# Differences of halves moved between the phases of a Strassen-like second MLP product, a residual update shared out over three doubled phases, and two loads of the first product moved by two steps

## The chip, the cores and the metric

One core of a Trainium2 chip runs the whole program. The metric is the device time of one execution in microseconds. Before the change it is 2566.15 us, the median of three runs (2564.7 to 2566.99). This kernel's runs differ by about 0.1% from each other.

## The reference, cut to what matters

The reference is one layer of an encoder over 2048 tokens of width 1024, in float32: a mixer of two attention kinds, then an MLP with a squared ReLU. The change lies in the MLP alone.

```python
h = rmsnorm(x, g_norm2[l]) * (1.0 + sc2) + sh2
x = x + gt2 * (jnp.square(jax.nn.relu(h @ w1[l])) @ w2[l])
```

`w1` is 1024 by 4096 and `w2` 4096 by 1024. Call `h @ w1` the first product, its squared ReLU the hidden layer, and the product with `w2` the second product.

## The kernel before, in words

**Numbers and tiles.** TensorE multiplies in pairs of float32r parts: each operand is split into a high and a low part (a cast on ScalarE, then a subtraction on VectorE), and each product is three matmuls (`mm3`). Both MLP products use a fast block scheme with seven block products in place of eight, numbered 1, 5, 6, 3, 7, 2, 4 in the order in which they run. The price is sums and differences of blocks, which run on VectorE. Tokens come in two halves (`mb` 1, then 0), each with two groups of 512 (`odd` 1 and 0).

**Steps.** The MLP is one list `steps`. A step is twelve matmuls in the first product (`First`) and in a plain phase (`Second`), six in a doubled phase (`Outer`). Everything that TensorE doesn't do is put into `jobs` by `at(n, job)`: job `n` is written out just ahead of step `n`. Before each step the loop (line 1978) also splits operands for later steps, as long as the eight tiles of `opp` suffice. Each engine then works its own instructions off in that order; the DMA queue of SyncE does so too, so that a DMA that waits holds up all that are written behind it. A table of step numbers, written by hand, thus sets the order on VectorE and in the DMA queue.

**The first product, `mb` 0.** For each of 16 column pairs `j` there are seven steps (a period). VectorE splits the next operands (`opw`), forms three sums of weight blocks for the next pair in temporary tiles (`ts`), combines four finished blocks (`cp`, `ca`, `cb`, `ce`), and prepares sums of `w2` for later phases (`wt`). For `j` below 8 it also makes four differences between the two token halves, for the block products 3, 7, 2 and 4. `other(i)` (line 1560) loads the other half's block from `scr_hid` into a temporary tile `to`; `keep` (line 1551) subtracts in place and stores the tile to `scr_hid` two steps later. Temporary tiles (`temp`) come from a pool of seven; a `ts` of the next period takes the memory of a `to` of the last one, and so waits until that `to` has been stored. Up to the eighth period an update of the residual also runs for the other half (`xu`: load a row of `scr_x`, add, store), in the two tiles of `rp`.

**The second product, `mb` 0.** It runs as: a plain phase for block product 1 (16 steps), doubled phase 7, a plain phase for 6 (16 steps), and doubled phases 5, 2, 3 and 4. A doubled phase takes one of the seven block products and applies the scheme a second time inside it: seven parts of eight steps, in the order 1, 5, 6, 3, 7, 2, 4. For each step VectorE subtracts the low part of one operand `opr`, and in every second step one `ol`. Its right operands `r` (four tiles for each part, `half` and `half_sum`, lines 1790 and 1796) are loaded for parts 1, 5, 3 and 2, and computed as differences for parts 6, 7 and 4: `6 = 3 - 5`, `7 = 6 - 1`, `4 = 2 - 6`. For doubled phase 5 part 5 is a difference as well (`5 - 1`). At the end of a part VectorE adds the finished sums from PSUM into rows of the residual (`txo`, `cxo`): four such additions where the phase serves two outputs (7 and 5), two elsewhere. `update` (line 1641) adds the sums of the plain phases to rows that no doubled phase finishes (`txu`): load, add six steps later, store three steps later.

**The numbers in the plan.** `plan["load"]` and `plan["sum"]` (lines 1916 to 1932) give for each part the step of the first of its four tiles and the gap between them. They are made for the phase that comes next: `f` is the first step of the phase just laid out, `e` the step behind its last one. In the first plan `f` is the plain phase for 1, so `f + 16` is the first step of doubled phase 7. In the plan that doubled phase 7 makes for doubled phase 5, `e` is the first step of the plain phase for 6 and `e + 16` that of doubled phase 5.

Of the kernel before, what the change touches and what calls it, by code (L numbers as in the profile page):

```python
# [79 lines left out]
def encoder_kernel(ctx, tc, xT, c, g1, g2, w_in, w_rest, gqk, bias, w_o, w1, w2, w_ada, b_ada, out):  # L80
# [1215 lines left out]
    if True:  # L1296
# [37 lines left out]
        def at(n, job):  # L1334
            jobs.setdefault(n, []).append(job)
# [228 lines left out]
        def second_sums(j, step):  # L1564

            t = []

            def load():
                t.append(raw_pair([P, 2, 2, TB], F32, f"w2s_{j}"))
                for s in range(2):  # L1570
                    sp.dma_start(t[0][:, s].rearrange("p r n -> p (r n)"), w2[2 * j + s])

            def out(i, dst, a, b, op):
                tile = {nm: t[0][:, s, r, :] for nm, s, r in (("11", 0, 0), ("21", 0, 1), ("12", 1, 0), ("22", 1, 1))}
                column_sum(dve, tile[dst], tile[a], tile[b], op)
                later.add(2, lambda: sp.dma_start(scr_s[i - 1 if i < 7 else 0, j // 2][:, j % 2, :], tile[dst]))

            at(step - (6 if j else 0), load)
            sums = ((5, "22", "21", "22", ALU.add), (7, "21", "11", "21", ALU.subtract))
            sums += ((6, "11", "22", "11", ALU.subtract), (3, "12", "12", "11", ALU.subtract))  # L1580
            for n, x in enumerate(sums):
                at(step + n + (0 if j else 3), lambda x=x: out(*x))
# [51 lines left out]
        def weigh(x, a, n):  # L1634
            dve.scalar_tensor_tensor(x, a, mod[:, 5 * KT + n : 5 * KT + n + 1], x, op0=ALU.mult, op1=ALU.add)

        def rows_of(t, mb, n, odd):
            tb = 2 * mb + odd
            return t[n * P : (n + 1) * P, tb * TB : (tb + 1) * TB]

        def update(mb, r, odd, loads, adds, home=None, last=False):

            xs = {}

            def fetch(n):
                xs[n] = x = (home or temp)(f"xu{mb}_{r}{odd}_{n}")
                sp.dma_start(x, scr_x[2 * mb + odd, HK * r + n])

            def add(n):
                x, row = xs[n], HK * r + n  # L1650
                weigh(x, Second.whole["s", n], row)
                dst = rows_of(out, mb, row, odd) if last else scr_x[2 * mb + odd, row]
                later.add(3, lambda: sp.dma_start(dst, x))

            for n in range(HK):
                at(loads[n], lambda n=n: fetch(n))
                at(adds[n], lambda n=n: add(n))

        def plain(mb, i):

            f = len(steps)
            steps.extend(Second(mb, i, j) for j in range(NP))
            if i == 6:
                spread = lambda *ns: [f + n for n in ns]
                update(mb, 0, 1, spread(0, 1, 2, 8), spread(4, 5, 6, 12))
            return f
# [27 lines left out]
        def narrow_sums(i, k, step):  # L1694

            t = []
            r, s = {2: (0, 1), 4: (1, 1)}[i]

            def load():
                for a in range(2):  # L1700
                    t.append(temp(f"wn{i}_{k}_{a}"))
                    sp.dma_start(t[a], w2[2 * (HP * a + k) + s][:, r * TB : (r + 1) * TB])

            def sums(pr, dst, a, b, op):
                v = {nm: t[h][:, c * CN : (c + 1) * CN] for nm, h, c in (("11", 0, 0), ("12", 1, 0), ("21", 0, 1), ("22", 1, 1))}
                column_sum(dve, v[dst], v[a], v[b], op)
                later.add(2, lambda: sp.dma_start(scr_t[i, pr][:, k, :], v[dst]))

            at(step - 4, load)
            todo = ((5, "22", "21", "22", ALU.add), (7, "21", "11", "21", ALU.subtract))  # L1710
            todo += ((6, "11", "22", "11", ALU.subtract), (3, "12", "12", "11", ALU.subtract))
            for n, x in enumerate(todo):
                at(step + n, lambda x=x: sums(*x))
# [154 lines left out]
        for mb in (1, 0):  # L1868
            begin = len(steps)
            steps += [First(mb, j, i) for j in range(NP) for i in OUTER]  # L1870
            end = len(steps)
            for j in range(NP):
                f = steps[begin + 7 * j]
                if mb:
                    second_sums(j, begin + 7 * j + 2)
                    if j >= HP:
                        narrow_sums(2, j - HP, begin + 71 + 5 * (j - HP))
                else:
                    outer_sums((7, 5, 3, 4)[j // 4], j % 4, begin + 7 * j - 2)
                    if j < HP:  # L1880
                        for i, n in ((3, 2), (2, 5), (7, 2), (4, 5)):
                            at(begin + 7 * j + n, lambda i=i, f=f: f.other(i))
                if j > mb:
                    at(begin + max(7 * j - 13, 2 if mb else -6), f.load)
                if j > mb or mb and j:
                    for m in range(4):
                        at(begin + (m + 1 if mb and j == 1 else 7 * j - 9 + (m if j > 1 else 0)), lambda f=f, m=m: f.fetch(m))
            if mb:
                norm2(1, begin + 18)
                norm2(0, begin + 48)  # L1890
                for k in range(HK):
                    begins = end + 6 * k
                    pieces = right_blocks(0, k, kept if k % 2 else temp)
                    for n, m in ((0, 0), (4, 4), (5, 5), (6, 6), (7, 7), (8, 7), (9, 7), (10, 7), (11, 7), (12, 7)):
                        at(begins + n, pieces[m])
                for i in PLAIN:
                    plain(1, i)
                for n in range(end, len(steps), 2):
                    at(n - 7 - max(0, end + 4 - n) // 2, steps[n].load)
                rest = len(steps)  # L1900
                lent = lambda nm: rp.tile([P, TB], F32, tag="r", name=nm)
                for n, (r, odd) in enumerate(((0, 0), (1, 1), (1, 0))):
                    at_row = rest + 3 + 16 * n
                    update(1, r, odd, range(at_row, at_row + 16, 4), range(at_row + 4, at_row + 20, 4), lent)
            else:
                at(begin - 8, steps[begin].load)
                at(begin - 6, steps[begin].fetch)

        def plain_loads(f, leads):
            for m in range(0, NP, 2):  # L1910
                at(f + m - (leads.pop(0) if leads else 7), steps[f + m].load)

        f = plain(0, 1)
        plain_loads(f, [9, 9, 9, 8, 8, 8])
        e = len(steps)
        plan = {"load": {1: (f - 3, 1), 5: (f + 2, 2), 3: (f + 10, 2), 2: (f + 18, 2)}}
        plan["sum"] = {6: (f + 16, 2), 7: (f + 21, 2), 4: (f + 44, 2)}
        for i in DOUBLE:
            f = outer(i, plan)
            e = len(steps)  # L1920
            if i == 7:
                plain_loads(plain(0, 6), [12, 11, 11, 11, 9, 8])
            spread = lambda *ns: [f + n for n in ns]
            if i == 2:
                update(0, 0, 0, spread(18, 22, 26, 30), spread(24, 28, 32, 36))
                update(0, 1, 1, spread(36, 40, 44, 48), spread(42, 46, 50, 54))
            if i == 3:
                update(0, 1, 0, spread(12, 16, 20, 24), spread(17, 21, 25, 29), None, True)
            plan = {"load": {1: (f + 22, 2), 5: (f + 17, 2), 3: (f + 30, 2), 2: (f + 46, 2)}}
            plan["sum"] = {6: ({7: e + 1, 5: e - 4}.get(i, f + 38), 2), 7: (e + (8 if i == 7 else 16), 2), 4: (e + (16 if i == 7 else 26), 2)}  # L1930
            if i == 7:
                plan["sum"][5] = (f + 31, 2)

        blocks = [right_blocks(1, k, kept if k else temp) for k in range(HK)]

# [104 lines left out]
```

## Time and profile before

| what | number |
|---|---|
| median of three runs | 2566.15 us |
| the profiled execution, its own time | 2567.03 us |
| its span, first to last instruction | 2565.3 us |
| TensorE busy (matmuls) | 2523.2 us, 98% |
| TensorE weight loads busy | 2094.1 us, 82% |
| VectorE busy | 2054.8 us, 80% |
| ScalarE busy | 1509.6 us, 59% |
| GpSimd busy | 747.5 us, 29% |
| DMA of SyncE, share of 16 engines | 80.4% |
| granted TensorE clock, mean | 0.999 |

All recorded operations have line L42, that of the helper which keeps them in program order, so the profile is read by tile names, not by lines. Times are given from the start of the span. A busy share tells what an engine did on average; how much a stage loses is read from the stage itself, by the time that it takes against the time of its matmuls when nothing holds them up. The MLP's first product for `mb` 0 begins at 1757 us, its second product at 2075 us, and the last matmul ends at 2561 us.

### The profile page before, as it was taken

To read this page: it belongs to the slowest core of one execution; us is meant where nothing else is said; L and a number is where in the kernel's file an instruction comes from. 1 tells how busy PE (TensorE), PEld (TensorE's weight loads), DVE (VectorE), ACT (ScalarE), POOL (GpSimd) and SP (SyncE) were. 2 spreads that over 40 slices of the span, in tenths; PEclk is the share of its full clock that TensorE was granted. 3 is DMA by queue.
4 is the path that set the end of the run, shared out by engine and by line. 5 is a ranking of instruction groups with operands and counts; after the bars stand their busy time and mean duration, and the time that the engine had idled before them with its cause. 6 is when DMAs were issued, how large, how long until landed. Compare 5 with 4: busy or idle time off the path is not lost.

```text
span 2565.3 us, 39482 instructions
## 1 busy us (share of the span) xinstructions
PE 2523.2 (98%) x12388; PEld 2094.1 (82%) x12388; DVE 2054.8 (80%) x3593; ACT 1509.6 (59%) x2893; POOL 747.5 (29%) x1128
## 2 busy tenths in 40 slices
PE   9999999999999999999999999999999999999999
PEld 7888888888888888887988888888778887787777
DVE  7656767887789879998768777789777659899998
ACT  6333435668866686666745555575445546466665
POOL 4330144776776667776710000000000000000000
PEclk9999999999999999999999999999999999999999
DMA  9879979789977788866787879987998886868892
GB/s 364 325 296 361 341 280 296 212 236 289 278 250 234 226 262 271 258 208 198 227 332 246 309 268 316 347 320 244 324 325 289 270 338 263 321 254 291 282 314 81
DMA packets 305105, 714.66 MB, mean 279 GB/s; under 512 B 32512, under 2 KB 91904, under 8 KB 293248
## 3 DMA queue, kind: packets, MB, share of 16 engines
q1 hardware_dynamic: 303600, 707.43, 80.4%
q10 hardware_dynamic: 1296, 4.72, 0.5%
q8 instruction: 98, 1.61, 0.3%
q14 instruction: 111, 0.91, 0.1%
HBM read 485.00 MB, written 227.02 MB: 278 GB/s over the span
## 4 chain that ended last, share of the span: by engine, by line
PE 71%; DVE 14%; DMA 7%; ACT 3%; issue 3%; POOL 1%; SPq 0%; DVEq 0%; ACTq 0%; POOLq 0%
PE ps L42 19%; PE pt L42 11%; PE ps_s L42 10%; PE acc L42 6%; PE wt L42 6%; PE pf L42 4%; PE z L42 4%; PE po L42 4%; DVE opr L42 3%; PE pq L42 3%; DVE r L42 2%; DVE p L42 2%; DMA scr_t<-wt 1%; PE cz L42 1%; DMA scr_hid<-to 1%
## 5 line engine op out<-in xcount | busy, mean ns | idle before, releaser
L42 PE MATMUL ps<-h,opw 128*128 128x512 f32 x1512 | 358.6, 389 | 0.0
L42 ACT CAST wth<-wt 128x512 fp32r<-128x512 f32 (+3 forms) x544 | 257.1, 483 | 167.7 <-PE wt L42 158.4
L42 POOL TENSOR_TENSOR b<-p 128x512 f32<-128x512 f32 (+1 forms) x320 | 292.5, 914 | 167.8 <-DVE p L42 93.0
L42 DVE TENSOR_TENSOR wtl<-wt,wth 128x512 fp32r<-128x512 f32 (+3 forms) x544 | 291.0, 547 | 58.1 <-ACT wth L42 56.3
L42 PEld LDWEIGHTS ps<-h,opw 128*128 128x128 f32 x1512 | 283.7, 188 | 58.8
L42 PE MATMUL ps_s<-h,opw 128*128 128x512 f32 x1152 | 278.5, 391 | 11.0 <-DVE cp L42 8.1
L42 PE MATMUL pt<-w,ht 128*128 128x512 f32 x1248 | 288.2, 391 | 0.0
L42 PEld LDWEIGHTS pt<-w,ht 128*128 128x128 f32 x1248 | 233.0, 188 | 47.7
L42 DVE TENSOR_TENSOR_SCAN p<-z,p,zero 128x512 f32<-128x512 f32 x192 | 245.7, 1281 | 25.6 <-ACT z L42 18.5
L42 PEld LDWEIGHTS ps_s<-h,opw 128*128 128x128 f32 x1152 | 215.2, 188 | 59.8 <-DVE cp L42 11.0
L42 ACT CAST opr<-r 128x512 fp32r<-128x512 f32 x280 | 174.2, 623 | 146.0 <-PE ps L42 69.7
L42 PE MATMUL ps<-opr,ol 128*128 128x512 f32 x960 | 223.6, 391 | 2.3 <-DVE opr L42 1.9
L42 PE MATMUL acc<-wth,v 128*128 128x512 f32 (+3 forms) x544 | 220.9, 410 | 0.0
L42 PEld LDWEIGHTS ps<-opr,ol 128*128 128x128 f32 x960 | 179.2, 188 | 44.2 <-DVE opr L42 5.3
L42 DVE TENSOR_TENSOR opr<-r,opr 128x512 fp32r<-128x512 f32 x280 | 185.8, 686 | 18.3 <-ACT opr L42 17.0
L42 ACT ACTIVATE z<-z 128x512 f32<-128x512 f32 (+1 forms) x320 | 166.5, 521 | 55.4 <-PE z L42 49.0
L42 PE MATMUL z<-k,q 128*128 128x512 f32 (+3 forms) x640 | 185.6, 372 | 7.7 <-DVE p L42 7.0
L42 PE MATMUL acc<-wtl,v 128*128 128x512 f32 (+3 forms) x544 | 185.7, 348 | 0.0
L42 PE MATMUL ps_s<-opr,ol 128*128 128x512 f32 x720 | 172.9, 394 | 4.7 <-DVE opr L42 3.9
L42 PE MATMUL ps<-oph,opv 128*128 128x512 f32 x768 | 176.0, 390 | 0.6 <-DVE oph L42 0.2
L42 PE MATMUL wt<-ident,b 128*128 128x128 f32 x1088 | 171.4, 273 | 0.9 <-DVE p L42 0.6
L42 PEld LDWEIGHTS ps<-oph,opv 128*128 128x128 f32 x768 | 143.9, 188 | 32.2 <-DVE oph L42 1.2
(215 smaller groups left out, 4875.1 us busy)
## 6 DMA issues: line engine op xcount, KB each, us to landing
r<-scr_hid SPq DMA_DIRECT2D x80, 512.0 KB, 7.3
q<-scr_q SPq DMA_DIRECT2D x128, 256.0 KB, 5.2
w<-in_w_dram SPq DMA_DIRECT2D x64, 512.0 KB, 5.8
k<-scr_k SPq DMA_DIRECT2D x240, 128.0 KB, 4.4
v<-scr_v SPq DMA_DIRECT2D x120, 256.0 KB, 4.1
wa<-in_w_ada_dram SPq DMA_DIRECT2D x48, 512.0 KB, 6.2
ow<-scr_wo SPq DMA_DIRECT2D x24, 1024.0 KB, 6.0
l<-scr_t SPq DMA_DIRECT2D x20, 1024.0 KB, 7.9
```

The source lines that it names most:

```text
L42: return lambda *x, **y: self.tc.keep_in_program_order(f(*x, **y))
```

## The change

It alters numbers in the table and moves two calls.

- First product: the loads for differences 3 and 7 are put two steps later (step 4 of the period in place of step 2).
- First plan: the loads for parts 5 and 3 and the differences for parts 6 and 7 of doubled phase 7 are put earlier.
- Plan for doubled phase 5: its own part-5 differences move from step 31 of doubled phase 7 to the first steps of the plain phase for 6; parts 6, 7 and 4 follow later.
- Updates: one row group (`odd` 1) moves from doubled phase 2 to doubled phase 3, another (`odd` 0) from 3 to 4.

```diff
-                        for i, n in ((3, 2), (2, 5), (7, 2), (4, 5)):
+                        for i, n in ((3, 4), (2, 5), (7, 4), (4, 5)):
                             at(begin + 7 * j + n, lambda i=i, f=f: f.other(i))
...
-        plan = {"load": {1: (f - 3, 1), 5: (f + 2, 2), 3: (f + 10, 2), 2: (f + 18, 2)}}
-        plan["sum"] = {6: (f + 16, 2), 7: (f + 21, 2), 4: (f + 44, 2)}
+        plan = {"load": {1: (f - 3, 1), 5: (f + 1, 2), 3: (f + 6, 2), 2: (f + 18, 2)}}
+        plan["sum"] = {6: (f + 12, 2), 7: (f + 15, 2), 4: (f + 44, 2)}
...
             if i == 2:
                 update(0, 0, 0, spread(18, 22, 26, 30), spread(24, 28, 32, 36))
-                update(0, 1, 1, spread(36, 40, 44, 48), spread(42, 46, 50, 54))
+                pass
             if i == 3:
-                update(0, 1, 0, spread(12, 16, 20, 24), spread(17, 21, 25, 29), None, True)
+                update(0, 1, 1, spread(18, 22, 26, 30), spread(24, 28, 32, 36))
+            if i == 4:
+                update(0, 1, 0, spread(2, 6, 10, 14), spread(8, 12, 16, 20), None, True)
...
-            plan["sum"] = {6: ({7: e + 1, 5: e - 4}.get(i, f + 38), 2), 7: (e + (8 if i == 7 else 16), 2), 4: (e + (16 if i == 7 else 26), 2)}
+            plan["sum"] = {6: ({7: e + 8, 5: e - 4}.get(i, f + 38), 2), 7: (e + (20 if i == 7 else 16), 2), 4: (e + (30 if i == 7 else 26), 2)}
             if i == 7:
-                plan["sum"][5] = (f + 31, 2)
+                plan["sum"][5] = (e + 1, 2)
```

TensorE's and ScalarE's instructions keep their order. Three places show what moves.

The DMA queue of SyncE in the fourth period (`j` = 3) of the first product, as one piece of the difference. `to0_3_1_3` is the tile of period 3 for difference 3; a row that begins with `scr_hid0` is the store of a finished difference, here of period 2.

```order
 L42 DMA xu1_11_1_21769<-scr_x3_5_217 128x512
-L42 DMA to0_3_1_3_21771<-scr_hid1_3_1_16881 128x512
-L42 DMA to0_3_1_7_21773<-scr_hid1_7_1_16913 128x512
-L42 DMA scr_hid0_7_1_16849<-to0_2_1_7_21593 128x512
-L42 DMA scr_hid0_3_1_16817<-to0_2_1_3_21591 128x512
+L42 DMA scr_hid0_7_1_16849<-to0_2_1_7_21632 128x512
+L42 DMA scr_hid0_3_1_16817<-to0_2_1_3_21630 128x512
 L42 DMA scr_t7_3_16772<-wt7_3_21503 128x2x256
 L42 DMA scr_hid0_4_1_16825<-to0_2_1_4_21658 128x512
+L42 DMA to0_3_1_3_21809<-scr_hid1_3_1_16881 128x512
+L42 DMA to0_3_1_7_21811<-scr_hid1_7_1_16913 128x512
 L42 DMA scr_x3_4_216<-xu1_11_0_21654 128x512
```

The two loads go behind the stores of differences 7, 3 and 4; what follows keeps its place.

VectorE in doubled phase 7, part 7, before the change, and then with it. `r5_5_1` is a part-5 difference for doubled phase 5, `r7_4_2` a part-4 difference for phase 7 itself.

```order
L42 TENSOR_TENSOR opr7_7_4_24666<-r7_7_2_24365,opr7_7_4_24666 128x512
L42 TENSOR_TENSOR ol7_7_4_24669<-l7_7_0_24512,ol7_7_4_24669 128x512
L42 TENSOR_TENSOR r7_4_2_24672<-r7_2_2_24321,r7_6_2_24294 128x1024
L42 TENSOR_TENSOR opr7_7_5_24686<-r7_7_2_24365,opr7_7_5_24686 128x512
L42 TENSOR_TENSOR r5_5_1_24498<-r5_5_1_24498,r5_1_1_24566 128x1024
L42 TENSOR_TENSOR opr7_7_6_24696<-r7_7_3_24396,opr7_7_6_24696 128x512
L42 TENSOR_TENSOR ol7_7_6_24699<-l7_7_0_24512,ol7_7_6_24699 128x512
L42 TENSOR_TENSOR r7_4_3_24702<-r7_2_3_24352,r7_6_3_24323 128x1024
L42 TENSOR_TENSOR opr7_7_7_24712<-r7_7_3_24396,opr7_7_7_24712 128x512
L42 TENSOR_TENSOR r5_5_2_24523<-r5_5_2_24523,r5_1_2_24589 128x1024
```

```order
L42 TENSOR_TENSOR opr7_7_4_24665<-r7_7_2_24288,opr7_7_4_24665 128x512
L42 TENSOR_TENSOR ol7_7_4_24668<-l7_7_0_24512,ol7_7_4_24668 128x512
L42 TENSOR_TENSOR r7_4_2_24671<-r7_2_2_24329,r7_6_2_24248 128x1024
L42 TENSOR_TENSOR opr7_7_5_24685<-r7_7_2_24288,opr7_7_5_24685 128x512
L42 TENSOR_TENSOR opr7_7_6_24694<-r7_7_3_24315,opr7_7_6_24694 128x512
L42 TENSOR_TENSOR ol7_7_6_24697<-l7_7_0_24512,ol7_7_6_24697 128x512
L42 TENSOR_TENSOR r7_4_3_24700<-r7_2_3_24356,r7_6_3_24277 128x1024
L42 TENSOR_TENSOR opr7_7_7_24710<-r7_7_3_24315,opr7_7_7_24710 128x512
```

Two of the four part-5 differences for phase 5 stood in these rows, the others just ahead of and behind them; all four now stand in the plain phase for 6.

VectorE in doubled phase 5, at the change from part 5 to part 6, before the change and then with it. `cxo` adds finished sums from PSUM.

```order
L42 TENSOR_TENSOR opr5_5_7_25490<-r5_5_3_24548,opr5_5_7_25490 128x512
L42 TENSOR_TENSOR opr5_6_0_25507<-r5_6_0_25035,opr5_6_0_25507 128x512
L42 TENSOR_TENSOR ol5_6_0_25510<-l5_6_0_25403,ol5_6_0_25510 128x512
L42 TENSOR_TENSOR opr5_6_1_25521<-r5_6_0_25035,opr5_6_1_25521 128x512
L42 TENSOR_TENSOR opr5_6_2_25530<-r5_6_1_25078,opr5_6_2_25530 128x512
L42 TENSOR_TENSOR ol5_6_2_25533<-l5_6_0_25403,ol5_6_2_25533 128x512
```

```order
L42 TENSOR_TENSOR r5_7_3_25474<-r5_6_3_25299,r5_1_3_24619 128x1024
L42 TENSOR_TENSOR opr5_5_7_25482<-r5_5_3_24548,opr5_5_7_25482 128x512
L42 TENSOR_TENSOR opr5_6_0_25499<-r5_6_0_25184,opr5_6_0_25499 128x512
L42 TENSOR_TENSOR ol5_6_0_25502<-l5_6_0_25391,ol5_6_0_25502 128x512
L42 TENSOR_TENSOR opr5_6_1_25513<-r5_6_0_25184,opr5_6_1_25513 128x512
L42 TENSOR_TENSOR opr5_6_2_25522<-r5_6_1_25223,opr5_6_2_25522 128x512
L42 TENSOR_TENSOR ol5_6_2_25525<-l5_6_0_25391,ol5_6_2_25525 128x512
L42 TENSOR_TENSOR r5_4_0_25528<-r5_2_0_24864,r5_6_0_25184 128x1024
```

Doubled phase 5 now holds its four part-7 differences, which stood in the plain phase for 6, and its part-4 differences stand some steps later than before.

## The prediction

> **What bounds the kernel now.** I read the page first: TensorE is busy for 98% of the span at full clock, so what can be won is the little that it idles. Then I cut the MLP's last part into stretches and asked for each one's length. In the rows below stand the stretch, its length, the busy time of TensorE, its weight loads, VectorE, ScalarE and GpSimd, the clock, the DMA share and GB/s. After the page's row, the first seven are periods of the first product (`j` = 3 to 9), then come the plain phase for 1, doubled phase 7, the plain phase for 6, and doubled phases 5, 2, 3 and 4.
>
> ```profile
> PE 2523.2 (98%) x12388; PEld 2094.1 (82%) x12388; DVE 2054.8 (80%) x3593; ACT 1509.6 (59%) x2893; POOL 747.5 (29%) x1128
> ...
> 1814.49:1836.40 21.91, 19.67 (x86) 15.61 (x84) 16.25 (x26) 10.23 (x18) 0.00 (x0) 1.00 0.91 315
> 1836.40:1859.24 22.84, 19.69 (x86) 15.61 (x84) 16.82 (x27) 10.22 (x18) 0.00 (x0) 1.00 0.99 347
> 1859.24:1879.97 20.73, 19.35 (x85) 15.69 (x84) 16.91 (x27) 10.01 (x18) 0.00 (x0) 1.00 0.99 340
> 1879.97:1900.35 20.38, 19.35 (x86) 15.69 (x85) 16.82 (x27) 10.01 (x18) 0.00 (x0) 1.00 0.91 294
> 1900.35:1921.36 21.01, 19.33 (x86) 15.69 (x84) 16.25 (x26) 10.02 (x18) 0.00 (x0) 1.00 0.99 335
> 1921.36:1941.55 20.19, 19.33 (x85) 15.69 (x84) 16.14 (x27) 10.01 (x18) 0.00 (x0) 1.00 0.98 338
> 1941.55:1960.59 19.04, 19.04 (x85) 15.77 (x84) 13.45 (x22) 10.23 (x18) 0.00 (x0) 1.00 0.81 276
> 2075.00:2118.52 43.52, 43.52 (x193) 36.05 (x193) 23.04 (x36) 21.29 (x38) 0.00 (x0) 1.00 0.88 346
> 2118.52:2202.04 83.52, 80.37 (x337) 62.22 (x337) 82.17 (x121) 50.76 (x87) 0.00 (x0) 1.00 0.75 283
> 2202.04:2245.90 43.86, 43.82 (x193) 35.96 (x193) 35.48 (x51) 18.27 (x32) 0.00 (x0) 1.00 0.83 325
> 2245.90:2322.06 76.16, 76.16 (x337) 63.06 (x337) 72.37 (x112) 50.46 (x86) 0.00 (x0) 1.00 0.74 270
> 2322.06:2403.88 81.82, 79.34 (x337) 62.27 (x337) 80.64 (x119) 50.41 (x86) 0.00 (x0) 1.00 0.78 268
> 2403.88:2483.99 80.11, 79.00 (x337) 62.30 (x337) 76.66 (x116) 50.00 (x86) 0.00 (x0) 1.00 0.90 307
> 2483.99:2561.05 77.06, 76.74 (x336) 62.56 (x335) 66.82 (x101) 46.93 (x80) 0.00 (x0) 1.00 0.39 132
> ```
>
> A period that nothing holds up takes 19.04 us, a doubled phase 76.16, a plain phase 43.52. So the six periods from 1814 to 1942 lose 127.06 - 6 x 19.04 = 12.8 us, and doubled phases 7, 5, 2, 3 and 4 lose 7.4, 0, 5.7, 3.9 and 0.9 us: 17.9 together. These are the two losses that the change can touch.
>
> The **doubled phases** lose where VectorE has no idle time left (82.17 of 83.52 us busy). Its instructions there, start by start (start, duration, and in brackets idle time before and its cause):
>
> ```profile
> 2163.49 1.22 DVE L42 TENSOR_TENSOR r<-r,r 128x1024 f32<-128x1024 f32 x1
> 2164.62 0.68 DVE L42 TENSOR_TENSOR opr<-r,opr 128x512 fp32r<-128x512 f32 x1
> 2165.22 1.21 DVE L42 TENSOR_TENSOR r<-r,r 128x1024 f32<-128x1024 f32 x1
> 2166.36 2.72 DVE L42 SCALAR_TENSOR_TENSOR txo<-ps,mod,txo 128x512 f32<-128x512 f32 x4
> 2169.00 0.68 DVE L42 TENSOR_TENSOR opr<-r,opr 128x512 fp32r<-128x512 f32 x1
> ...
> 2129.39:2140.59 11.20, 11.20 (x50) 1.00 1.04 416
> 2140.59:2152.49 11.90, 11.65 (x49) 1.00 1.04 411
> 2152.49:2163.37 10.88, 10.88 (x49) 1.00 0.35 139
> 2163.37:2177.58 14.21, 12.62 (x49) 1.00 0.67 235
> 2177.58:2191.15 13.57, 12.26 (x50) 1.00 0.73 260
> ```
>
> From start to start a split costs 0.60, a difference 1.14, an addition from PSUM 2.64 / 4 = 0.66. The lower five rows are parts 5, 6, 3, 7 and 2 of phase 7 (length, TensorE busy, clock, DMA share, GB/s); the third, unhindered, takes 10.88. I counted VectorE's instructions for each part in the program's order. Part 7 has 9 splits, 4 additions and 6 differences: 5.4 + 2.6 + 6.8 = 14.9 us, and takes 14.2. All seven come to 10.0, 11.2, 11.7, 10.4, 14.9, 13.4, 10.5, an excess over 10.88 of 7.6 in sum, against 7.4 lost. The same count gives 5.0 for phase 2, 3.9 for phase 3, 0.5 for phase 4 and 0 for phase 5. That is 17.0 against 17.9: what a part has too much is lost, and a light part hardly pays for a heavy one.
>
> The **first product** loses through a store. The waits of VectorE, then one of them and the matmuls behind it:
>
> ```profile
> DVE ts L42 <- DMA scr_hid<-to: 27.4, 7, 5.2
> ...
> 1840.65 0.69 DVE L42 TENSOR_TENSOR ts<-w 128x512 f32<-128x512 f32 x1 [5.22 <-DMA scr_hid<-to]
> ...
> 1849.01 3.03 PE L42 MATMUL ps_s<-h,opw 128*128 128x512 f32 x12 [1.57 <-ACT cp L42]
> 1856.34 1.90 PE L42 MATMUL ps_s<-h,opw 128*128 128x512 f32 x7 [1.58 <-DVE cp L42]
> ```
>
> The next pair's weight sum `ts` waits until difference 3 has left the memory that it takes; VectorE's whole queue stands behind it, and TensorE runs dry some steps on. The store's own place in the DMA queue:
>
> ```profile
> 1824.77 1.29 DVE L42 TENSOR_TENSOR to<-cp,to 128x512 f32<-128x512 f32 x2
> ...
> 1831.59 0.32 SPq L42 DMA_DIRECT2D xu<-scr_x  x1
> 1832.28 0.81 SPq L42 DMA_DIRECT2D to<-scr_hid  x2
> 1833.16 1.52 SPq L42 DMA_DIRECT2D scr_hid<-to  x2
> 1835.58 0.37 SPq L42 DMA_DIRECT2D scr_t<-wt  x1
> ...
> 1847.59 1.29 DVE L42 TENSOR_TENSOR to<-cp,to 128x512 f32<-128x512 f32 x2
> ```
>
> Differences 7 and 3 were made by 1826.06, but their stores went out at 1833.16 to 1834.68, behind two loads that VectorE uses only at 1847.59.
>
> **The change, part by part.**
>
> *Phase 7.* Three differences go into the plain phase ahead and four (those for phase 5) into the plain phase behind. VectorE is busy there for 23.04 of 43.52 and 35.48 of 43.86 us, so 3 x 1.14 = 3.4 more in the one is hidden; the other gives up as many as it takes, four. My count of the parts becomes 10.0, 10.8, 9.9, 10.9, 10.9, 11.1, 10.5: 0.2 over. Gain 7.6 - 0.2, scaled to what was lost: 7.1. At its start the differences stand closer, 5 differences and 7 splits (9.9 us) within five steps (6.8). The cover is VectorE's lead there:
>
> ```profile
> 2113.77 1.30 DVE L42 TENSOR_TENSOR opr<-r,opr 128x512 fp32r<-128x512 f32 x2 [1.42 <-ACT opr L42]
> ...
> 2119.69 0.69 DVE L42 TENSOR_TENSOR opr<-r,opr 128x512 fp32r<-128x512 f32 x1 [1.91 <-ACT opr L42]
> ```
>
> The split at 2119.69 is for step 4, which TensorE begins at 2118.52 + 4 x 1.36 = 2123.96: 3.6 us after it is done, against 3.1 too much. I take 0, and 3.1 as the price if that lead is gone. The loads that go ahead with them pass loads of the plain phase by a place each, with VectorE waiting for none there; 0.
>
> *Phase 5.* It gets the four part-7 differences, 4.6 us. Parts 6 and 3 come to 11.5 and 11.7: 0.6 + 0.8 = 1.4 lost. The lower end is 0, since its other parts are light and the phase in all holds 75.7 of 76.16; the upper end is 2.4, if each part also pays for being late at its additions.
>
> *Updates.* Each has four additions of 0.66, one load and one store per row. In phase 2 parts 2 and 4 get lighter (13.2 to 12.5, 11.1 to 10.4): gain 0.9. In phase 3 the parts over 10.88 were 12.0, 12.7 and 11.9 and become 13.4 and 12.5: loss 0.2. In phase 4, so far nearly free, parts 3 and 7 become 12.0 and 12.0 instead of 10.8 and 11.4: loss 1.7. Together -1.0; between +0.8 (phase totals of 78.4, 74.8 and 68.5 us, only the first over 76.16) and -2. The moved loads keep six steps of lead, and phase 4 has DMA to spare (share 0.39).
>
> Doubled phases: 7.1 - 1.4 - 1.0 = 4.7; I take **5.0**, a little toward the phase totals, whose excess falls from 5.8 + 3.6 to 2.2, that is by 7.2. Bounds 1 (7.1 - 3.1 - 2.4 - 2 gives -0.4, but not all at once) and 7.5.
>
> *First product.* The stores of 7 and 3 take the loads' places, so the second goes out by 1833.09 instead of 1834.68: 1.6 us. If every period gains that, capped by what it loses (2.87, 3.80, 1.69, 1.34, 1.97, 1.15), it is 1.6 + 1.6 + 1.6 + 1.34 + 1.6 + 1.15 = 8.9. But the DMA share of these periods is 0.99, 0.99, 0.99 and 0.98 in four of six. Weighted over 127.06 us it is 0.96, so 4.8 us of DMA time are free; with one shift of 1.6 the most is 6.4. If DMA throughput alone sets the period, the shift counts once: 1.6. I take **3.5**, nearer the low end, as most rows are near 0.99: the two periods at 0.91 gain 1.6 and 1.34, the rest 0.6. The loads go out five places later, some 5 us; from issue to landing the DMAs of `to` took 5.9 in the median:
>
> ```profile
> DMA to landing us min/median/max: 3.1/5.9/8.6
> ```
>
> In period 3 they then land near 1843, 4 us ahead of use.
>
> The Trainium skill, "DMA: Bandwidth & Descriptors", section Bandwidth, puts HBM traffic of one core at about 358 GB/s. By it the six periods' 41.7 MB (length by GB/s) could pass in 117 us, and the most to win would be 10.5 instead of 6.4. The trace doesn't bear that bound out: 416 GB/s stand in the row at 2129.39, and a share of 0.99 at 335 to 347 GB/s in the periods.
>
> The sum: 5.0 + 3.5 = 8.5 us off the span of 2565.3, which lies 1.7 below its execution's own 2567.03; that lies 0.9 above the median. So 2567.03 - 8.5 = 2558.5 for such an execution, **2557.6** for the median.
>
> **The rivals.**
>
> *One shift only in the first product* (DMA throughput sets the period). For it: four shares near 0.99. Against: two at 0.91, where the queue stood still. Gain 5.0 + 1.6 = 6.6: 2559.5.
>
> *The moved work is lost again elsewhere.* The burst in phase 7 costs 3.1, phase 5 loses 2.4, the updates 2.0: 7.1 - 7.5 = -0.4, with 1.6 from the first product, so 2565. For it: phases 2 and 3 lost somewhat more than the count. Against: phase 5 before has idle time, and the lead at 2119.69.
>
> *Slower: the late loads become the wait.* If a load of `to` lands after its use, VectorE's queue stands there, in up to eight periods. In periods 1 and 5 the loads now also go behind an `xu` load that holds the DMA queue until its tile is stored. Period 5, the `xu` load and the first use:
>
> ```profile
> 1881.19 0.32 SPq L42 DMA_DIRECT2D xu<-scr_x  x1
> ...
> 1888.73 1.29 DVE L42 TENSOR_TENSOR to<-cp,to 128x512 f32<-128x512 f32 x2
> ```
>
> Sent near 1881.6 and landed 3.1 to 8.6 us later, 5.9 in the median, they come at 1887.5, 1.2 us ahead of use; from a landing time of 7.1 on, this rival decides. If the queue falls back so far that each of eight periods waits 2 us, the price is 16 us, less the 5.0 of the doubled phases, and the first product gains nothing: 11 us slower, 2577. Against: in the other periods 4 us are left, and the `xu` load itself gets free earlier, since its store moves up by two places.
>
> *No change at all* from the order would need VectorE not to be the limit; its 82.17 of 83.52 us speak against it.
>
> **How the numbers follow.** Forecast 50%, one shift 22%, lost again 18%, slower 8%, something unnamed 2%. A measurement of this kernel can tell about 0.2%, 5.1 us, from no change: faster means below 2561.0. The forecast is faster nearly always (0.48), one shift mostly (0.20), lost again seldom (0.04), with some of the unnamed: 0.73. Slower is the third rival, 0.08; 0.19 are left for the same. The forecast's own range is 2553.5 to 2561; with the upper bounds (7.5 + 6.4 = 13.9, 2552.2) and most of the second rival it is 2552 to 2565.
>
> **What would show it.** In the profile of the changed kernel: phase 7 near 76.4 us with part 7 and part 2 near 10.9; phase 5 near 77.5; phases 2 and 3 near 80 to 81; phase 4 near 78.5; `ts` still waiting for stores of `to`, but 12 to 20 us in sum, and the six periods near 123.5 us. Wrong would be: phase 5 or 4 losing over 3 us, waits of `to` on loads, or the six periods unchanged.

## The result, and the profile after

The changed kernel takes 2557.67 us (median of seven runs, 2556.39 to 2559.33), the kernel before 2566.15 (seven runs, 2564.7 to 2567.45). The ratio is 0.9967, with a 95% interval of 0.9955 to 0.9979: 8.5 us faster, 5.4 to 11.5. The forecast was 2557.6.

The profiled execution took 2558.36 us, with a span of 2556.6. Its page row first:

```profile
PE 2520.1 (99%) x12388; PEld 2095.2 (82%) x12388; DVE 2055.6 (80%) x3593; ACT 1510.6 (59%) x2893; POOL 746.0 (29%) x1128
```

The busy times are those of before within some us, since no work was taken away. The stretches tell more, with the same columns as before: six periods of the first product (`j` = 3 to 8), then doubled phases 7, 5, 2, 3 and 4.

```profile
1816.20:1835.44 19.24, 19.24 (x85) 15.69 (x85) 16.32 (x26) 10.02 (x18) 0.00 (x0) 1.00 0.99 344
1835.44:1856.31 20.87, 19.36 (x85) 15.69 (x85) 16.82 (x27) 10.01 (x18) 0.00 (x0) 1.00 0.99 335
1856.31:1875.76 19.45, 19.35 (x86) 15.70 (x85) 16.92 (x27) 10.11 (x18) 0.00 (x0) 1.00 0.99 362
1875.76:1896.34 20.58, 19.33 (x85) 15.69 (x85) 17.00 (x27) 10.01 (x18) 0.00 (x0) 1.00 0.94 310
1896.34:1917.18 20.84, 19.37 (x85) 15.69 (x85) 16.32 (x26) 10.01 (x18) 0.00 (x0) 1.00 0.98 337
1917.18:1937.88 20.70, 19.34 (x86) 15.70 (x85) 16.40 (x27) 10.04 (x18) 0.00 (x0) 1.00 0.98 333
...
2114.68:2191.66 76.98, 76.88 (x337) 62.82 (x337) 75.06 (x115) 50.81 (x87) 0.00 (x0) 1.00 0.81 306
2235.52:2313.38 77.86, 77.14 (x338) 62.84 (x337) 76.20 (x116) 50.44 (x86) 0.00 (x0) 1.00 0.73 264
2313.38:2393.90 80.52, 78.74 (x338) 62.28 (x337) 79.33 (x118) 50.40 (x86) 0.00 (x0) 1.00 0.79 276
2393.90:2474.01 80.11, 78.35 (x338) 62.43 (x337) 75.75 (x114) 50.39 (x86) 0.00 (x0) 1.00 0.82 277
2474.01:2552.38 78.37, 77.58 (x337) 62.41 (x335) 69.17 (x105) 46.90 (x80) 0.00 (x0) 1.00 0.49 157
```

| stage | before, us | after, us | gain | forecast of the gain |
|---|---|---|---|---|
| six periods of the first product | 127.06 | 121.68 | 5.4 | 3.5 |
| doubled phase 7 | 83.52 | 76.98 | 6.5 | 7.1 |
| doubled phase 5 | 76.16 | 77.86 | -1.7 | -1.4 |
| doubled phase 2 | 81.82 | 80.52 | 1.3 | 0.9 |
| doubled phase 3 | 80.11 | 80.11 | 0.0 | -0.2 |
| doubled phase 4 | 77.06 | 78.37 | -1.3 | -1.7 |

The gains come to 10.2 us, and the span is 8.7 shorter. The rest is no part of the change: the first product for `mb` 0 began at 1757.49 us in the one profiled execution and at 1759.06 in the other, 1.57 later, though the program up to there is the same.

Inside doubled phases 7 and 5 the rows are those of parts 7 and 2 of phase 7 and of parts 5, 6 and 3 of phase 5 in the changed kernel:

```profile
2158.20:2169.48 11.28, 11.28 (x49) 8.86 (x49) 11.28 (x17) 7.07 (x12) 0.00 (x0) 1.00 0.75 260
2169.48:2180.78 11.30, 11.20 (x49) 8.92 (x49) 11.30 (x20) 7.06 (x12) 0.00 (x0) 1.00 0.95 319
2246.40:2257.28 10.88, 10.88 (x50) 9.01 (x49) 10.88 (x16) 7.45 (x13) 0.00 (x0) 1.00 0.90 351
2257.28:2268.29 11.01, 11.01 (x50) 8.93 (x49) 11.01 (x17) 7.07 (x12) 0.00 (x0) 1.00 0.59 215
2268.29:2280.74 12.45, 11.72 (x50) 8.85 (x49) 12.45 (x21) 7.06 (x12) 0.00 (x0) 1.00 0.28 85
```

Part 7 of phase 7 took 14.21 us and takes 11.28, part 2 took 13.57 and takes 11.30. VectorE (the third time with a count) is busy for every bit of each of these five stretches. In phase 5, part 3 now takes 12.45 in place of 10.88: that is nearly all that phase 5 loses.

What is left in the first product stands in the waits (waiting tile, releaser, us in total, times, longest). VectorE's, in the changed kernel from 1757 to 2072 us, has one row with a DMA:

```profile
DVE ts L42 <- DMA scr_hid<-to: 20.4, 12, 4.2
```

There is no wait of `to` on its load. The stores are still waited for, for 20.4 us in place of 27.4. In the DMA queue of SyncE, from 1797 to 1938 us, the longest wait is this one, first in the kernel before and then in the changed one:

```profile
SPq L42 <- DMA scr_x<-xu: 22.6, 10, 4.3
```

```profile
SPq L42 <- DMA scr_x<-xu: 18.2, 9, 3.2
```

A load of `xu` stands at the head of the queue until the row before it, in the same tile, has been stored to `scr_x`. Everything that is written behind it, the stores of differences among it, waits along. The queue of the changed kernel in period 4 (start, duration, operation):

```profile
1835.14 0.32 SPq L42 DMA_DIRECT2D scr_x<-xu  x1
1835.68 0.32 SPq L42 DMA_DIRECT2D scr_hid<-to  x1
1837.10 0.85 SPq L42 DMA_DIRECT2D to<-scr_hid  x2
1840.62 0.32 SPq L42 DMA_DIRECT2D xu<-scr_x  x1
1840.99 0.90 SPq L42 DMA_DIRECT2D wt<-scr_s  x2
```

From 1837.95 to 1840.62 the queue issues nothing: one of the nine waits, for the store of a row to land.

What the moved loads themselves do is seen one period earlier, in period 3, where no such wait stands between the `xu` load and the stores of differences 7 and 3:

```profile
1829.70 0.32 SPq L42 DMA_DIRECT2D xu<-scr_x  x1
1830.28 0.87 SPq L42 DMA_DIRECT2D scr_hid<-to  x2
```

From the issue of the `xu` load until the second store is issued it takes 1.45 us (1829.70 to 1831.15). In the kernel before it took 3.09 (1831.59 to 1834.68, in the prediction's rows), with the two loads in between: the shift of 1.6 us that the forecast counts is there.

### The profile page after: what moved, and what is told of

Read it like the earlier page. It is cut to its first block, busy times and chain, and to the rows that moved or that the text cites. A ratio compares the mean times of both kernels' runs of the same rounds, so it can differ in the third digit from the quotient of the medians.

```text
span 2556.6 us, 39502 instructions
## 1 busy us (share of the span) xinstructions
PE 2520.1 (99%) x12388; PEld 2095.2 (82%) x12388; DVE 2055.6 (80%) x3593; ACT 1510.6 (59%) x2893; POOL 746.0 (29%) x1128
## 4 chain that ended last, share of the span: by engine, by line
PE 74%; DVE 14%; DMA 4%; ACT 3%; issue 3%; POOL 1%; SPq 0%; DVEq 0%; ACTq 0%; POOLq 0%
PE ps L42 21%; PE ps_s L42 11%; PE pt L42 11%; PE acc L42 6%; PE wt L42 6%; PE pf L42 4%; PE z L42 4%; PE po L42 4%; PE pq L42 3%; DVE opr L42 3%; DVE r L42 2%; DVE p L42 2%; PE cz L42 1%; DVE ol L42 1%; DVE txo L42 1%
```

## The experiments

Each time is the median of its runs; the ratios are against runs of the kernel before on the same chip. For the first product the loss of the six periods over 6 x 19.04 us is given from the profile, for the second product the lengths of the doubled phases.

### The loads alone, and the second product alone

The kernel before with the one line of the loads:

```diff
-                        for i, n in ((3, 2), (2, 5), (7, 2), (4, 5)):
+                        for i, n in ((3, 4), (2, 5), (7, 4), (4, 5)):
```

> The kernel before with one edit: the loads for differences 3 and 7 of the first product two steps later. Theory 1 (each of the six slow periods of the first product gets its awaited store out earlier): the six periods fall from 127.1 us to 121 to 122, as in the changed kernel (121.7), the doubled phases stay as before, the time falls by 5 us to about 2561. Theory 2 (DMA throughput sets these periods, so one shift counts once): 125.5 us, the time falls by 1.6 to 2564.5.

And the changed kernel with that line put back:

```diff
-                        for i, n in ((3, 4), (2, 5), (7, 4), (4, 5)):
+                        for i, n in ((3, 2), (2, 5), (7, 2), (4, 5)):
```

> The changed kernel with the two loads put back to their old step, so that only the second product differs from the kernel before. Theory (the two parts of the change don't touch each other): the six periods of the first product take 127 us again, the doubled phases lose 13.2 us in sum as in the changed kernel against 18.0 before, the time is 4.8 us under the kernel before, about 2561.4. Rival (the second product gains because the first one leaves the DMA queue emptier): the doubled phases lose 15 us or more.

The loads alone took 2561.59 us, ratio 0.9985 (0.9976 to 0.9994): 3.8 us faster, 1.5 to 6.2. The second product alone took 2560.13, ratio 0.9982 (0.9974 to 0.9991): 4.6 us, 2.3 to 6.7. Together 8.4, what both give in one kernel. The six periods in one row each, first with the loads alone, then with the second product alone:

```profile
1813.24:1932.40 119.16, 115.79 (x505) 94.20 (x505) 99.43 (x160) 60.22 (x108) 0.00 (x0) 1.00 1.00 343
```

```profile
1814.19:1941.37 127.18, 116.72 (x505) 93.89 (x505) 99.47 (x160) 60.64 (x108) 0.00 (x0) 1.00 0.96 331
```

With the loads at their old place the six periods lose 12.9 us, as before (12.8); with the loads moved 4.9 here and 7.4 in the changed kernel. The doubled phases of the second run are those of the changed kernel within 0.2 us, phase by phase, and those of the first run those of before: the two parts of the change don't touch each other. The profile of the first run is its fastest execution of eleven (2557.74 us, 3.9 under its median). Its first product began 1.4 us earlier than in the profile of before, and what the six periods take in its other runs is not known, so its 7.9 us of gain there may be more than it gains in most of them.

Only the sum of the six periods can be compared from profile to profile, not one period: with the loads at step 2, period 6 took 20.4 us in the profile of before and 19.1 in that of the second product alone, where the sums are 127.06 and 127.18.

### The update rows out of the way

The changed kernel, with the rows of the residual update 56 steps later, behind period 8:

```diff
-                    at_row = rest + 3 + 16 * n
+                    at_row = rest + 59 + 16 * n
```

> The changed kernel with the residual update that runs beside the first product begun 56 steps later, in the periods without differences (12 loads and 12 stores of 256 KB each leave the six slow periods). Theory A (what is left of the loss, 7.4 us, is DMA traffic and a held DMA queue): the six periods fall from 121.7 us to 114.2 to 116, the later periods stay at 19.04, the time falls by 5.5 to 7.4 us to about 2551. Theory B (the awaited store's place in the queue alone sets the wait): the waits of the weight sums on the stores stay near 20 us and the time at 2557.

It took 2550.54 us, ratio 0.9942 (0.993 to 0.9955), some 7 us faster than the changed kernel. The six periods:

```profile
1816.60:1930.84 114.24, 114.24 (x505) 94.59 (x505) 94.22 (x151) 60.88 (x108) 0.00 (x0) 1.00 0.97 319
```

They are 6 x 19.04 us long: nothing is lost any more. But two causes went at once, the rows' bytes and the queue's wait for them.

### The same bytes, without the held queue

The changed kernel again, the rows at their place, but added one step earlier and stored one step sooner after that:

```diff
-        def update(mb, r, odd, loads, adds, home=None, last=False):
+        def update(mb, r, odd, loads, adds, home=None, last=False, wait=3):
...
-                later.add(3, lambda: sp.dma_start(dst, x))
+                later.add(wait, lambda: sp.dma_start(dst, x))
...
-                    update(1, r, odd, range(at_row, at_row + 16, 4), range(at_row + 4, at_row + 20, 4), lent)
+                    update(1, r, odd, range(at_row, at_row + 16, 4), range(at_row + 3, at_row + 19, 4), lent, wait=2)
```

> The changed kernel with the rows of the residual update stored two steps earlier in the first product (added after three steps in place of four, stored two steps later in place of three). The bytes in each period stay the same; what goes is that the next load of a row stands at the head of the DMA queue until the row before it in its tile has been stored (18.2 us of waits there between 1797 and 1938 us in the changed kernel). If those waits set the loss that is left in the first product, most of the 7.4 us goes, as it did with the rows late: six periods near 115 us, 2551 to 2553 in all. If the bytes set it, the periods stay near 121.7 us and the time near 2557.

It took 2549.58 us, ratio 0.9934 (0.9922 to 0.9947). Its first two periods of the six, all six in one row, and the queue's wait for `xu`:

```profile
1814.25:1833.29 19.04, 19.04 (x86) 15.77 (x85) 17.19 (x28) 10.12 (x18) 0.00 (x0) 1.00 1.06 371
1833.29:1852.33 19.04, 19.04 (x86) 15.77 (x85) 16.71 (x28) 10.12 (x18) 0.00 (x0) 1.00 1.04 373
```

```profile
1814.25:1928.49 114.24, 114.24 (x506) 94.59 (x505) 99.30 (x160) 60.72 (x108) 0.00 (x0) 1.00 1.02 357
```

```profile
SPq L42 <- DMA scr_x<-xu: 1.1, 3, 0.6
```

The wait fell from 18.2 to 1.1 us, and with it the whole loss. The bytes are the same: 114.24 us by 357 GB/s are 40.8 MB, 121.68 by 336 in the changed kernel 40.9. That row of the changed kernel:

```profile
1816.20:1937.88 121.68, 116.00 (x505) 94.14 (x505) 99.77 (x160) 60.21 (x108) 0.00 (x0) 1.00 0.98 336
```

So with the loads at step 4 it was the held queue, and the bytes alone set nothing. The edit also gives the stores of the rows an earlier place in the queue; no run separates that from the shorter wait.

### The kernel before, without the held queue

Two kernels ask what the order of loads and stores is worth without that wait. The kernel before with the rows late (the line of the third run), and the kernel before with the rows stored two steps earlier (the edit of the run above):

> The kernel before, with only the update rows of the first product 56 steps later, the loads of differences 3 and 7 still at step 2. If the rows are the whole cause, the loss of 12.8 us in the six periods goes here too, and the order of loads and stores is worth nothing by itself: near 2553. If loads ahead of stores cost something by themselves (1.6 us for each period at most, by the forecast), 2 to 8 us of loss stay: 2555 to 2561.

> The kernel before, with only the rows of the update stored two steps earlier; the loads of differences 3 and 7 stay at step 2, the second product is that of before. If the held DMA queue is the whole cause, the six periods lose nothing here either: 190.4 us from the start of the first product to period 10, and near 2554 in all, as with the rows late (2555.1). If loads ahead of the stores cost something by themselves once the rows are in the queue too, some of the 12.8 us stays: 2557 to 2562.

The first took 2555.1 us, ratio 0.9956 (0.9942 to 0.997), the second 2557.28, ratio 0.997 (0.9958 to 0.9982). The six periods of each:

```profile
1813.10:1927.34 114.24, 114.24 (x506) 94.60 (x505) 94.12 (x151) 60.89 (x108) 0.00 (x0) 1.00 0.96 315
```

```profile
1816.08:1933.70 117.62, 115.90 (x506) 94.13 (x505) 99.25 (x160) 60.16 (x108) 0.00 (x0) 1.00 1.00 347
```

| six periods lose, us | rows held | rows stored earlier | rows late |
|---|---|---|---|
| loads at step 2 | 12.8, 12.9 | 3.4 | 0.0 |
| loads at step 4 | 7.4, 5.6, 4.9 | 0.0 | 0.0 |

Neither cause is the whole. With the rows stored earlier the loads ahead of the stores still cost 3.4 us (the wait for `xu` is down to 2.7 us there); with the rows held, moving the loads saves 5.4 to 8.0. With the rows late, moving the loads is worth nothing. The first run's theory thus held in the periods, though its median is 2 us above the 2553 expected; the second run's theory, that the held queue explains all, fell.

What joins the two causes is the wait that the prediction named, that of `ts` on the stores of `to`. Here it is in the six periods alone, from the profile of each kernel:

| kernel | `ts` waits for stores, us | six periods lose, us |
|---|---|---|
| before | 24.2 | 12.8 |
| second product alone | 24.0 | 12.9 |
| changed kernel | 19.2 | 7.4 |
| changed, part-7 differences early (next section) | 18.0 | 5.6 |
| loads alone | 16.8 | 4.9 |
| before, rows stored earlier | 15.7 | 3.4 |
| changed, rows stored earlier | 12.5 | 0.0 |
| before, rows late | 10.1 | 0.0 |
| changed, rows late | 5.3 | 0.0 |

In the second row 5.1 us are put down to the store of an `xu` row. The two rebalanced kernels below wait 5.5 and 10.1 us and lose under 0.1. Up to 12.5 us of this wait cost nothing; where it is longer, all but 11 to 12.5 us of it is lost. Both edits act by shortening the same wait, and once it is inside what VectorE has to spare, shortening it further gains nothing.

### Do light parts pay for heavy ones?

The changed kernel, with the differences for parts 6 and 7 of phase 5 four and thirteen steps earlier, in the plain phase for 6:

```diff
-            plan["sum"] = {6: ({7: e + 8, 5: e - 4}.get(i, f + 38), 2), 7: (e + (20 if i == 7 else 16), 2), ...
+            plan["sum"] = {6: ({7: e + 4, 5: e - 4}.get(i, f + 38), 2), 7: (e + (7 if i == 7 else 16), 2), ...
```

> The changed kernel with the part-7 differences of doubled phase 5 back in the plain phase for 6. VectorE's work in phase 5 falls from 75.7 to 71.2 us, in its parts 1 and 5 (to 9.0 and 7.8), while parts 6 and 3 keep 11.5 and 11.7 against 10.88. Theory (what a part has too much is lost, whatever the parts before it hold): phase 5 still loses 1.4 to 1.7 us, the time stays at 2557.7. Rival (VectorE works ahead in light parts, and that pays for the heavy ones): phase 5 loses nothing, the time is 1.7 us lower, unless the plain phase, now at 38.8 of 43.5 us, loses it.

It took 2555.55 us, ratio 0.9961 (0.9947 to 0.9975), which its times can't tell from the changed kernel's 0.9967. Parts 5, 6 and 3 of phase 5 tell it:

```profile
2244.05:2254.93 10.88, 10.88 (x49) 9.01 (x48) 7.95 (x12) 7.45 (x14) 0.00 (x0) 1.00 0.92 358
2254.93:2265.94 11.01, 11.01 (x49) 8.93 (x48) 11.01 (x17) 7.08 (x13) 0.00 (x0) 1.00 0.47 173
2265.94:2278.39 12.45, 11.69 (x49) 8.85 (x48) 12.45 (x21) 7.05 (x13) 0.00 (x0) 1.00 0.27 85
```

VectorE has 2.9 us of idle time in part 5, right ahead of the heavy parts, where it had none; parts 6 and 3 take 11.01 and 12.45 us, to the hundredth what they took. The idle time ends with ScalarE's casts of the next operands (2.8 us in four waits), so VectorE doesn't get further ahead by it. A light part doesn't pay here for a heavy one behind it. What its profile gains comes from the first product, with the same program there; its six periods in one row:

```profile
1815.57:1935.43 119.86, 116.01 (x506) 94.14 (x505) 99.70 (x160) 60.25 (x108) 0.00 (x0) 1.00 0.99 343
```

### All of it together

If the rule of parts holds, differences and updates can be put where the parts are light. The kernel with late rows, and beside it:

```diff
-                update(0, 0, 0, spread(18, 22, 26, 30), spread(24, 28, 32, 36))
+                update(0, 0, 0, spread(4, 28, 34, 38), spread(10, 34, 40, 44))
...
-                update(0, 1, 1, spread(18, 22, 26, 30), spread(24, 28, 32, 36))
+                update(0, 1, 1, spread(28, 35, 38, 44), spread(34, 41, 44, 50))
...
-                update(0, 1, 0, spread(2, 6, 10, 14), spread(8, 12, 16, 20), None, True)
+                update(0, 1, 0, spread(30, 34, 38, 42), spread(36, 40, 44, 48), None, True)
...
-            plan["sum"] = {6: ({7: e + 8, 5: e - 4}.get(i, f + 38), 2), 7: (e + (20 if i == 7 else 16), 2), 4: (e + (30 if i == 7 else 26), 2)}
+            plan["sum"] = {6: ({7: e + 4, 5: e - 4}.get(i, e + 0), 2), 7: (e + (7 if i == 7 else 16), 2), 4: (e + (22 if i == 7 else 26), 2)}
```

> The changed kernel with the rows late (as in the run before, 2550.5 there) and with the differences and updates of the doubled phases put where the parts are light: phase 5's differences in the plain phase ahead and in its first parts, those for part 6 of phases 3 and 4 at the start of the phase itself, the updates spread about the middle and the end. By the rule of parts the excess over 10.88 falls from 12.1 to 4.1 (phase 7 1.6, of which the run with late rows lost none; phases 2, 3 and 4 0.8 each), so the doubled phases lose 3 to 5 us in place of 13.2 and the time is near 2542. If a light part cannot be filled in this way, because what is put at a phase's start is late for its use, phases 3 and 4 lose as much as before: 2548 or more.

It took 2539.57 us, ratio 0.9894 (0.9881 to 0.9908): 27 us faster than before. Doubled phases 7, 5, 2, 3 and 4:

```profile
2105.85:2182.81 76.96, 76.86 (x338) 62.83 (x337) 75.05 (x115) 50.82 (x87) 0.00 (x0) 1.00 0.81 304
2226.69:2302.85 76.16, 76.16 (x337) 63.06 (x337) 72.26 (x112) 50.45 (x86) 0.00 (x0) 1.00 0.74 268
2302.85:2380.30 77.45, 77.14 (x337) 62.75 (x337) 75.58 (x115) 50.43 (x86) 0.00 (x0) 1.00 0.83 292
2380.30:2457.33 77.03, 76.72 (x338) 62.91 (x337) 75.28 (x114) 50.45 (x86) 0.00 (x0) 1.00 0.79 277
2457.33:2534.53 77.20, 76.73 (x337) 62.57 (x335) 72.33 (x109) 46.91 (x80) 0.00 (x0) 1.00 0.49 165
```

They lose 0.8, 0, 1.3, 0.9 and 1.0 us: 4.0, within the 3 to 5 expected, where the changed kernel loses 13.0. Beside them the period of the first product in which the late rows run lost 1.5 us (`j` = 11):

```profile
1965.66:1986.17 20.51, 19.37 (x86) 15.68 (x85) 13.86 (x23) 10.10 (x18) 0.00 (x0) 1.00 0.85 296
```

In the two other profiles with late rows this period lost 0 and 0.3 us, so the 1.5 is not a steady loss.

The last kernel has the same second product, with the rows at their old place and stored earlier:

> The rebalanced kernel (2539.57 us), with the rows at their old place and stored two steps earlier, in place of the late rows. If the hold alone was the cause, the first product loses nothing in the six periods, and the 1.5 us that the rebalanced kernel lost in period 11, where the late rows ran, goes too: 2537 to 2540. If the bytes of the rows matter, the first product loses 3 us or more: 2542 or above.

It took 2540.59 us, ratio 0.9906 (0.9894 to 0.9919), just above the 2537 to 2540 expected. In its profile period 11 is back at 19.04 us, and the six periods take 114.29. Its time can't be told from the one above; by their ratios both beat the changed kernel by 16 to 19 us.

## Why the forecast held, and where it did not

**Doubled phases: right, at 4.8 us for 5.0.** The rule "what a part has too much is lost, and a light part hardly pays for a heavy one" carried the sum, and three runs confirm it: the phases come out the same in each profile that has them, phase 5 lost as much with a light part ahead, and the rebalanced kernel gained 9.0 where the count of the excess (12.1 to 4.1) says 8.0. Its terms were off by less than a microsecond. Phase 7 gained 6.5 for 7.1: parts 7 and 2 were near 11.3 rather than 10.9. Phase 5 lost 1.7 for 1.4, with nearly all of it in part 3: the count put 0.6 in part 6 and 0.8 in part 3, and 0.1 and 1.6 were lost there. So the sum of neighbouring heavy parts is what the rule gives, not the share of each.

**Updates: 0.0 for -1.0.** Phase 2 gained 0.4 more than its count, and phases 3 and 4 lost 0.2 and 0.4 less. Phases 2, 3 and 4 differ between the two kernels by the updates alone, so this comes straight from their rows.

**The burst at phase 7's start: nothing, as taken.** Its first two parts took 10.88 us each; the price of 3.1 didn't come up. That VectorE comes out of the plain phase with a lead would explain it, but no run takes that lead away.

**First product: the mechanism right, the sum behind its size not.** The stores did take the loads' places, 1.6 us sooner in period 3, and `ts` waits for them less (20.4 us over the whole first product, just outside the 12 to 20 named). The term of 3.5 measured 5.4 in the profiles of the two kernels, and 5.4 to 8.0 by any pair of a moved and an unmoved profile. By times alone it is 3.8 (1.5 to 6.2), which doesn't tell 3.5 from 5.4; whether 3.5 was too small in most runs stays open. What failed is the step that held it down: "with one shift of 1.6 the most is 6.4", from 4.8 us of free DMA time, and the choice "nearer the low end, as most rows are near 0.99". That cap doesn't hold. Two profiles with the loads moved gain 7.2 and 7.9 (119.86 and 119.16 us in place of 127.06), and the same bytes pass in 114.24 us once the queue isn't held. A DMA share of 0.99 was read as a full DMA, while the queue that issues the transfers stood still for 22.6 of 141 us, in ten waits for one kind of store. The prediction's own row of 416 GB/s in phase 7 spoke against that reading too. The Trainium skill would have warned here: "Perfetto Trace Analysis", section Engine Utilization, says that a single active core may pull more than the 358 GB/s of its share, up to some 435 by its 16 DMA engines. The 371 and 373 GB/s of two periods without the held queue agree with it.

I did see the `xu` load that holds the queue, but only as a danger to the late loads, in the rival. I never asked what it costs as it stood, and it was worth more than the whole edit of the loads.

**The rivals.** One shift only, 1.6 us in the first product, fell by the profiles (5.4 and more; the times alone, 1.5 to 6.2, barely leave it in), and its ground, DMA throughput that sets the period, fell with the same bytes in 114.24 us. Lost again elsewhere fell: of its 7.1 us, phase 5 cost 1.7, the updates 0 and the burst 0. The slower one, late loads as the new wait, fell: VectorE waited for no load of `to` in the changed kernel.

**The total hit the median by 0.1 us, partly by luck.** The stages gained 10.2 in the two profiles, 1.7 more than forecast, and the first product happened to begin 1.57 later in the second of them. Over many runs the parts give 3.8 + 4.6 = 8.4.

## What to carry to other kernels

A transfer that waits for its buffer holds all that is written behind it in the same queue, so look first in the queue's own waits for loads that stand until a store has landed; two steps of earlier storing were worth 8 us here, as much as the whole change. Where one engine fills fixed windows of another, count its work window by window: the excess of each heavy window is lost, and idle time in the window ahead didn't help here, where the lead is short. A DMA share near 1 shows that transfers are under way, not that no more would go through; test it by changing the order at the same bytes.

## What the runs showed of the hardware

The DMA share can exceed 1 over whole periods (1.06 at 371 GB/s, 1.04 at 373), as it did over two parts of phase 7 before the change (1.04 at 416 and 411). Not expected: a share near 1 doesn't measure what is left. The same bytes (40.9 and 40.8 MB) passed at a share of 0.98 in 121.68 us and at 1.02 in 114.24.

The first product for `mb` 0 began between 1755.49 and 1759.43 us in eleven profiled executions whose programs are the same up to there. These 3.9 us of scatter lie ahead of all the edits, and are half of what the change gains: single profiles of this kernel can be compared stage by stage, but not by their ends. The doubled phases, in contrast, repeat within 0.2 us from profile to profile. What scatters upstream was not looked into.
